# Folding the 64-token turns of a two-layer decoder trunk: Silu, product and split moved to later pieces of weights

## The chip, the cores and the metric

The kernel runs on one core of one Trainium2 chip. The metric is the time of one execution on the device, in microseconds. TensorE (PE in the profile, its weight loads PEld), VectorE (DVE), ScalarE (ACT) and the queue that issues the DMAs (SP) each run their own list of instructions in order and meet through semaphores.

## The reference, cut to what matters

The program computes two decoder layers over 256 tokens of width 1024 in float32. The change touches the last block alone, a top-2-of-8 expert SwiGLU with 3584 hidden units to an expert:

```python
def swiglu(t, w_gate, w_up, w_down):
    return (jax.nn.silu(t @ w_gate) * (t @ w_up)) @ w_down

def moe_swiglu(t, router, w_gate, w_up, w_down):
    ...
    for e in range(N_EXPERTS):
        out = out + combine[:, e:e + 1] * swiglu(t, w_gate[e], w_up[e], w_down[e])
```

All products keep float32 accuracy: every weight and every hidden value is split into a high part (rounded to the float32r format) and a low part (what the rounding left), and the products of the parts are added up.

## The kernel before

**Turns.** The experts are ordered by their token counts and take turns, alternately a large turn (L, up to 128 tokens) and a small one (S, up to 64 tokens): `KIND = "LSLSLSLS"`. Each turn goes through 7 chunks of 512 hidden units. A chunk takes twelve pieces of weights of 128x1024: eight in `gate_up` (four for the gate, then four for the up product, here g0 to g7) and four in `down` (f0 to f3). The order on the engines is software-pipelined: `gate_up` of the next chunk, then `down` of this one, then `gate_up` of the one after.

**A piece.** `split_raw` splits it: ScalarE casts the high part `whi` (L189), VectorE subtracts the low part `wlo` (L190). Both lie in the pool `whl`, with three buffers each. `piece()` splits the piece two ahead before it hands out the next one. So in program order the split of g2 stands ahead of TensorE's products of g0; and as the third buffer is that of the piece just used, this cast waits until TensorE has read the high part of f3, the piece before g0. In an S turn a piece takes four matmuls of 512 columns (`mm2`, L1480 and L1481: the high part, the low part, twice), in an L turn six (`mm3`, L193 to L195).

**The fold of an S turn.** In S turns the left operand holds 64 tokens' high parts in columns 0 to 63 and their low parts in columns 64 to 127, so that two matmuls do what three do in an L turn. The sum of the two halves is then owed. It is done per chunk by `fold`: ScalarE copies the gate and up sums out of PSUM (L1503), TensorE turns and adds the halves with 16 matmuls against the matrix `fold` (`turned`, L1524), ScalarE takes Silu (L1528), VectorE multiplies (the product, L1531), and the result is split into the hidden operand `mhh`: ScalarE's cast (the high part, L189), VectorE's subtraction (the low part, L190). There are 28 folds, seven in each of the four S turns.

**When a step runs.** `after(n, f)` puts a step on a list; `tick()` is called after each piece's products and runs what is due. For a fold made at the end of a `gate_up`, ticks 1 to 4 come after f0 to f3 of the `down` that follows, ticks 5 to 12 after g0 to g7 of the next `gate_up`. The hidden operand of this fold is read in the `down` behind that. The other guest of these ticks is `combine`, which at the start of each turn adds the finished turn's result to `h` (casts `yh`, subtractions `yl`, sums into `h` at L1581), and `dispatch`, which gathers the next turn's tokens during the last `down` but one (`sel`, `xT`, `x`, `sT`). The first fold of an S turn falls into the last `down` of the L turn before it, the last one into the `down` with the dispatch of the L turn behind it.

`in_order` ties the instructions of each of TensorE, ScalarE and VectorE to the order of the program.

Of the kernel before, what the change touches and what calls it, by code (L numbers as in the profile page):

```python
# [10 lines left out]
F32 = mybir.dt.float32  # L11
# [6 lines left out]
OP = mybir.AluOpType  # L18
# [93 lines left out]
def _build(tc, nc, es, I, out, dbg, upto):  # L112
# [28 lines left out]
    def ps(shape, name, tag="ps"):  # L141
        return banks[tag].tile(shape, F32, name=name, tag=tag)
# [45 lines left out]
    def split_to(hi, lo, src):  # L188
        nc.scalar.copy(out=hi, in_=src)  # L189
        nc.vector.tensor_tensor(out=lo, in0=src, in1=hi.bitcast(F32), op=OP.subtract)  # L190
# [25 lines left out]
    def C(k):  # L216
        for offs, t in ((_COFF, cst), (_LOFF, csl), (_KOFF, csk)):
            if k in offs:
                o, n = offs[k]
                return t[:, o:o + n]  # L220
# [9 lines left out]
    def preload(func, after=None):  # L230

        after = eps if after is None else after.bitcast(F32)
        nc.scalar.activation(dummy, after, func, bias=eps, scale=0.0)
# [330 lines left out]
    with ExitStack() as l0:  # L564
# [272 lines left out]
        def finish(p, table=False):  # L837

            if not ya:
                ya.append(Blocks(4, "ya", b4))  # L840
            Yc = c4(Y[p])
            st = rt.tile([128, 3, 4], F32, name="st")
            nc.vector.tensor_scalar(st[:, 0, :], mv[p][:, :, 1], 64e-5, None, op0=OP.add)
            if table:
                nc.scalar.activation(st[:, 2, :], st[:, 0, :], AF.Sqrt)
            nc.vector.tensor_tensor(out=Yc, in0=Yc, in1=mv[p][:, :, 0:1].to_broadcast([128, 4, 64]), op=OP.subtract)
            if table:
                nc.vector.reciprocal(st[:, 2, :], st[:, 2, :])
            else:
                rsqrt(st[:, 2, :], st[:, 0, :], st[:, 1, :])  # L850
            bd = blockdiag("KR")[:, 0]
            for s in halves:
                nc.vector.tensor_tensor(out=bd[s, :, s], in0=Yc[s],
                                        in1=st[s, 2, :, None].to_broadcast([64, 4, 64]), op=OP.mult)
            yield
            g = ps([128, 4, 128], "yT", f"pp{p % 2}" if table else "ps")
            for c in range(4):
                nc.tensor.transpose(g[:, c, :], bd[:, c, :], ident)
            y_ = b1("yl")
            for s in halves:  # L860
                nc.vector.scalar_tensor_tensor(c4(y_[s]), g[s, :, s], V("lg", p)[s], c4(bonus[p][s]),
                                               op0=OP.mult, op1=OP.add)
            yield
            nc.vector.tensor_tensor(out=y_, in0=y_, in1=gg[p], op=OP.mult)
            hi, lo = ya[0](p)
            split_to(hi, lo, y_)
            yield
# [135 lines left out]
        end = [finish(2, True), finish(3, True)]  # L1003
# [21 lines left out]
    with ExitStack() as l0:  # L1025
# [47 lines left out]
        t = unp.tile([128, 2, D], F32, name="un")  # L1073
# [142 lines left out]
    t = unp.tile([128, 2, D], F32, name="un")  # L1216
# [140 lines left out]
    def experts(kinds, late=None, hook=None):  # L1357
# [6 lines left out]
        def after(n, f):  # L1364
            deferred.append([n, f])
# [117 lines left out]
        def gate_up(e, fc):  # L1483
            large = kinds[e] == "L"
            acc = []
            sums = {}
            for w in range(2):
                a = ps([128, 512], "gu", "gu")
                for i in range(4):
                    wh, wl = piece()  # L1490
                    for k in range(2):
                        kb = 2 * i + k
                        c = slice(k * 512, (k + 1) * 512)
                        if large:
                            mm3(a, (X[e][:, 0, kb, :], X[e][:, 1, kb, :]), (wh[:, c], wl[:, c]), kb == 0, kb == 7)
                        else:
                            mm2(a, X[e][:, kb, :], (wh[:, c], wl[:, c]), kb == 0, kb == 7)
                    tick()
                    next(side[0], None)
                acc.append(a)  # L1500
                if not large:
                    t = sums[w] = mt.tile([128, 512], F32, name=("msg", "mhl")[w], **({} if w else {"bufs": 1}))
                    after(1, lambda t=t, a=a: nc.scalar.copy(out=t, in_=a))  # L1503
            end = (e, fc) == (last, NFC - 1)
            if not large:
                return fold(sums, end)
            sgt = mt.tile([128, 512], F32, name="msg", bufs=1)
            nc.scalar.activation(sgt, acc[0], AF.Silu)
            if end:
                preload(AF.Sqrt)  # L1510
            nc.vector.tensor_tensor(out=sgt, in0=sgt, in1=acc[1], op=OP.mult)
            return sgt

        def fold(sums, end):

            H = mt.tile([128, 4, 128], F32R, name="mhh")
            t = mt.tile([128, 512], F32, name="mhl").rearrange("p (w f t) -> p w f t", w=2, f=4)
            pt = []

            def turned():  # L1520
                pt.append(ps([128, 2, 4, 64], "hT", "hT"))
                for w in range(2):
                    for f in range(4):
                        nc.tensor.matmul(pt[0][:, w, f, :], lhsT=sums[w][:, f * 128:(f + 1) * 128], rhs=C("fold"),  # L1524
                                         start=True, stop=True)

            def silu():
                nc.scalar.activation(t[:, 0], pt[0][:, 0], AF.Silu)  # L1528
                if end:
                    preload(AF.Sqrt)  # L1530
                nc.vector.tensor_tensor(out=t[:, 1], in0=t[:, 0], in1=pt[0][:, 1], op=OP.mult)  # L1531
            after(2, turned)
            after(3, silu)
            after(4, lambda: split_to(H[:, :, 0:64], H[:, :, 64:128], t[:, 1]))
            return H

        def hidden_T(sgt):
# [238 lines left out]
```

## Time and profile before

| | us |
|---|---|
| median of 3 runs | 1544.46 (1542.99 to 1547.32) |
| the profiled execution | 1547.44 |
| its span, from the first to the last instruction | 1545.6 |
| VectorE busy | 1251.6 (81%) |
| ScalarE busy | 1055.4 (68%) |
| TensorE busy, matmuls | 1465.9 (95%) |

A row of a timeline gives the start, the time busy, the engine, the line, the operation, what it writes and reads, and how many alike were merged; in brackets stands the idle time before it and what ended that. Neighbouring rows of one engine overlap by about 0.1 us, so the cost of an instruction in a full queue is read from start to start. "mhl" names three tiles in S turns: the copy of the up sums, and the tile with Silu and the product.

### The profile page before, as it was taken

Reading aid. Unit: us, or ns where it says so; the run is one execution under the profiler, and the core shown is the slowest. Engines: PE = TensorE matmul, PEld = TensorE weight load, DVE = VectorE, ACT = ScalarE, POOL = GpSimd, SP = SyncE. Lnnn points to the kernel's source line nnn. Section 1 sums busy time; section 2 is a strip of 40 time slices with the busy share of each in tenths; the row PEclk is TensorE's granted clock in tenths of the full one; section 3 lists DMA queues with packets and bytes.
Section 4 is the critical chain, followed back from the end, with each engine's and each line's share of the span. In section 5 each row is a group of like instructions: output and inputs, shape, how many; then the busy total and the mean of one; then the engine's idle time right before and its main releaser. Section 6 shows DMA issues by size and latency. Waiting matters only on the chain. (4 is left out here: it accounts for less than half of the span.)

```text
span 1545.6 us, 22475 instructions
## 1 busy us (share of the span) xinstructions
PE 1465.9 (95%) x7781; PEld 1190.0 (77%) x7781; DVE 1251.6 (81%) x1634; ACT 1055.4 (68%) x1440; POOL 85.6 (6%) x154
## 2 busy tenths in 40 slices
PE   7889899999999999999999999999999999999995
PEld 6879888998788887776677886677887668887663
DVE  6686865554576568989989989989998999998995
ACT  5644345444455568778887778888777887777884
POOL 4223110001010010000000000000000000000000
PEclk9999999999999999999999999999999999999997
DMA  8230025558553869999999999999998999999941
GB/s 292 76 105 19 1 94 182 186 181 290 161 190 123 312 222 352 340 332 353 409 374 364 381 353 342 391 406 358 354 376 323 384 409 354 363 376 332 369 185 32
DMA packets 78276, 426.86 MB, mean 276 GB/s; under 512 B 9200, under 2 KB 9472, under 8 KB 42560
## 3 DMA queue, kind: packets, MB, share of 16 engines
q1 hardware_dynamic: 77328, 422.38, 73.5%
q0 software_dynamic: 816, 2.87, 0.6%
q8 instruction: 65, 1.06, 0.3%
q14 instruction: 67, 0.55, 0.1%
HBM read 424.15 MB, written 1.05 MB: 275 GB/s over the span
## 5 line engine op out<-in xcount | busy, mean ns | idle before, releaser
L190 DVE TENSOR_TENSOR wlo<-mraw,whi 128x1024 fp32r<-128x1024 f32 x556 | 659.3, 1224 | 61.0 <-ACT whi L189 42.4
L189 ACT CAST whi<-mraw 128x1024 fp32r<-128x1024 f32 x556 | 574.3, 1050 | 123.3 <-PE gu L194 53.8
L190 DVE TENSOR_TENSOR wlo<-raw,whi 128x1024 fp32r<-128x1024 f32 x232 | 280.1, 1223 | 107.1 <-ACT whi L189 102.3
L189 ACT CAST whi<-raw 128x1024 fp32r<-128x1024 f32 x232 | 240.6, 1043 | 124.0 <-PE acc L194 37.9
L1481 PE MATMUL gu<-wlo,x 128*128 128x512 f32 x448 | 194.3, 434 | 21.1 <-DVE wlo L190 19.5
L195 PE MATMUL gu<-wlo,x 128*128 128x512 f32 x448 | 176.6, 394 | 2.1 <-DVE wlo L190 2.0
L1480 PE MATMUL gu<-whi,x 128*128 128x512 f32 x448 | 176.6, 394 | 0.0
L193 PE MATMUL gu<-whi,x 128*128 128x512 f32 x448 | 175.9, 393 | 0.1
L194 PE MATMUL gu<-whi,x 128*128 128x512 f32 x448 | 175.7, 392 | 0.1
L1481 PEld LDWEIGHTS gu<-wlo,x 128*128 128x128 f32 x448 | 83.9, 187 | 99.9 <-DVE wlo L190 86.1
L195 PEld LDWEIGHTS gu<-wlo,x 128*128 128x128 f32 x448 | 84.1, 188 | 25.2 <-DVE wlo L190 7.3
L193 PE MATMUL cp<-u,whi 128*128 128x256 f32 (+1 forms) x360 | 101.9, 283 | 0.0
L194 PE MATMUL cp<-u,wlo 128*128 128x256 f32 (+1 forms) x360 | 101.8, 283 | 0.0
L195 PE MATMUL cp<-u,whi 128*128 128x256 f32 (+1 forms) x360 | 101.8, 283 | 0.0
L193 PEld LDWEIGHTS gu<-whi,x 128*128 128x128 f32 x448 | 84.2, 188 | 18.9 <-ACT whi L189 0.8
L194 PEld LDWEIGHTS gu<-whi,x 128*128 128x128 f32 x448 | 84.2, 188 | 18.6 <-DVE x L190 0.4
L1481 PE MATMUL Y<-wlo,mhh 128*128 128x512 f32 x224 | 94.2, 421 | 3.6 <-DVE wlo L190 3.6
L1480 PE MATMUL Y<-whi,mhh 128*128 128x512 f32 x224 | 92.5, 413 | 2.7 <-DVE mhh L190 2.7
L1480 PEld LDWEIGHTS gu<-whi,x 128*128 128x128 f32 x448 | 84.4, 188 | 11.7
L193 PE MATMUL Y<-whi,mhh 128*128 128x512 f32 x224 | 91.6, 409 | 0.0
L195 PE MATMUL Y<-wlo,mhh 128*128 128x512 f32 x224 | 88.3, 394 | 0.8 <-DVE wlo L190 0.8
L194 PE MATMUL Y<-whi,mhl 128*128 128x512 f32 x224 | 87.7, 392 | 0.0
(435 smaller groups left out, 2461.7 us busy)
## 6 DMA issues: line engine op xcount, KB each, us to landing
mraw<-in_moe SPq DMA_DIRECT2D x277, 1024.0 KB, 6.9
raw<-in_moe SPq DMA_DIRECT2D x116, 512.0 KB, 6.5
raw<-in_ffn_gu SPq DMA_DIRECT2D x44, 512.0 KB, 3.4
raw<-in_w_in SPq DMA_DIRECT2D x38, 512.0 KB, 3.6
raw<-in_ffn_d SPq DMA_DIRECT2D x22, 512.0 KB, 3.5
raw<-in_w_out SPq DMA_DIRECT2D x16, 512.0 KB, 3.7
raw<-in_w_in SPq DMA_DIRECT2D x4, 416.0 KB, 9.3
h<-in_x SPq DMA_DIRECT2D x2, 512.0 KB, 6.7
```

The source lines that it names most:

```text
L189: nc.scalar.copy(out=hi, in_=src)
L190: nc.vector.tensor_tensor(out=lo, in0=src, in1=hi.bitcast(F32), op=OP.subtract)
L193: nc.tensor.matmul(o, lhsT=a[0], rhs=b[0], start=start, stop=False)
L194: nc.tensor.matmul(o, lhsT=a[1], rhs=b[0], start=False, stop=False)
L195: nc.tensor.matmul(o, lhsT=a[0], rhs=b[1], start=False, stop=stop)
L1480: nc.tensor.matmul(o, lhsT=a, rhs=b[0], start=start, stop=False)
L1481: nc.tensor.matmul(o, lhsT=a, rhs=b[1], start=False, stop=stop)
```

## The change

The one closure with Silu and product becomes two (`silu`, `times`), and the split becomes two (`high`, `low`). In every fold but the very last, the fold's matmuls run at tick 3 in place of 2, Silu at 5 in place of 3, the product at 6 in place of 3, the high part at 7 and the low part at 8 in place of 4. In the very last fold (`end`) the ticks stay as they are. No instruction is added, dropped or resized.

```diff
                 nc.scalar.activation(t[:, 0], pt[0][:, 0], AF.Silu)
                 if end:
                     preload(AF.Sqrt)
+
+            def times():
                 nc.vector.tensor_tensor(out=t[:, 1], in0=t[:, 0], in1=pt[0][:, 1], op=OP.mult)
-            after(2, turned)
-            after(3, silu)
-            after(4, lambda: split_to(H[:, :, 0:64], H[:, :, 64:128], t[:, 1]))
+
+            def high():
+                nc.scalar.copy(out=H[:, :, 0:64], in_=t[:, 1])
+
+            def low():
+                nc.vector.tensor_tensor(out=H[:, :, 64:128], in0=t[:, 1], in1=H[:, :, 0:64].bitcast(F32), op=OP.subtract)
+            for n, f in zip((2, 3, 3, 4, 4) if end else (3, 5, 6, 7, 8), (turned, silu, times, high, low)):
+                after(n, f)
             return H
```

## Rows read from the trace of the kernel before

**Rows 1.** The page's list of engines: busy time, share of the span, instructions.
```profile
PE 1465.9 (95%) x7781; PEld 1190.0 (77%) x7781; DVE 1251.6 (81%) x1634; ACT 1055.4 (68%) x1440; POOL 85.6 (6%) x154
```

**Rows 2.** Who waited for whom between 940 and 1045 us, most of the second S turn: us in total, times, the longest.
```profile
PEld gu L1481 <- DVE wlo L190: 18.8, 35, 1.2
DVE wlo L190 <- ACT whi L189: 7.2, 9, 1.4
ACT whi L189 <- PE gu L1480: 5.2, 10, 0.8
ACT mhl L1528 <- PE hT L1524: 5.2, 6, 1.0
PEld Y L1481 <- DVE wlo L190: 4.7, 11, 1.0
```

**Rows 3.** The same between 825 and 925 us, inside the second L turn.
```profile
ACT whi L189 <- PE gu L194: 15.1, 40, 0.8
ACT whi L189 <- PE Y L194: 9.2, 22, 2.1
DVE wlo L190 <- ACT whi L189: 3.6, 8, 1.9
PEld gu L195 <- DVE wlo L190: 0.2, 1, 0.2
```

**Rows 4.** The waits of SP's queue over the whole span, the first row.
```profile
SPq L1188 <- DVE wlo L190: 545.9, 244, 9.5
```

**Rows 5.** Busy time in stretches from one fold's first matmul to the next one's (for the first row, from one transpose to the next in an L turn): the stretch, its length, then PE, PEld, DVE, ACT and POOL with their instructions, granted clock, DMA share, GB/s.
```profile
871.20:888.10 16.90, 16.90 (x77) 13.89 (x76) 15.69 (x15) 13.47 (x15) 0.00 (x0) 1.00 0.98 375
939.60:957.90 18.30, 16.12 (x74) 11.95 (x73) 16.67 (x18) 14.83 (x19) 0.00 (x0) 1.00 0.97 346
957.90:974.40 16.50, 15.18 (x69) 11.02 (x68) 15.62 (x17) 13.41 (x16) 0.00 (x0) 1.00 0.96 354
974.40:989.70 15.30, 14.93 (x65) 10.10 (x64) 14.44 (x15) 13.50 (x17) 0.00 (x0) 1.00 0.97 403
989.70:1005.00 15.30, 14.91 (x65) 10.09 (x64) 14.42 (x15) 13.53 (x17) 0.00 (x0) 1.00 1.02 414
1005.00:1020.70 15.70, 14.93 (x66) 10.10 (x65) 14.84 (x17) 13.56 (x17) 0.00 (x0) 1.00 1.01 409
1039.30:1057.80 18.50, 18.02 (x89) 14.51 (x88) 16.76 (x17) 15.02 (x19) 0.00 (x0) 1.00 0.88 327
```

**Rows 6.** VectorE's timeline around one fold of the last S turn.
```profile
1450.06 5.79 DVE L190 TENSOR_TENSOR wlo<-mraw,whi 128x1024 fp32r<-128x1024 f32 x5
1455.76 0.42 DVE L1531 TENSOR_TENSOR mhl<-mhl,hT 128x256 f32<-128x256 f32 x1
1457.03 1.23 DVE L190 TENSOR_TENSOR wlo<-mraw,whi 128x1024 fp32r<-128x1024 f32 x1 [0.85 <-ACT whi L189]
1458.17 0.42 DVE L190 TENSOR_TENSOR mhh<-mhl,mhh 128x256 fp32r<-128x256 f32 x1
1458.51 10.33 DVE L190 TENSOR_TENSOR wlo<-mraw,whi 128x1024 fp32r<-128x1024 f32 x9
```

**Rows 7.** ScalarE's timeline around the same fold.
```profile
1452.40 1.99 ACT L189 CAST whi<-mraw 128x1024 fp32r<-128x1024 f32 x2
1455.20 0.39 ACT L1528 ACTIVATE mhl<-hT 128x256 f32<-128x256 f32 x1 [0.81 <-PE hT L1524]
1455.95 1.05 ACT L189 CAST whi<-mraw 128x1024 fp32r<-128x1024 f32 x1 [0.36 <-PE Y L1480]
1456.90 0.40 ACT L189 CAST mhh<-mhl 128x256 fp32r<-128x256 f32 x1
1457.21 2.94 ACT L189 CAST whi<-mraw 128x1024 fp32r<-128x1024 f32 x3
1460.56 2.18 ACT L189 CAST whi<-mraw 128x1024 fp32r<-128x1024 f32 x2 [0.41 <-PE gu L1480]
```

**Rows 8.** TensorE's timeline around the same fold: f1 up to 1453.27, the fold's matmuls, f2 from 1454.97; then g1's third and g2's second matmul.
```profile
1453.04 0.39 PE L1481 MATMUL Y<-wlo,mhh 128*128 128x512 f32 x1
1453.27 1.00 PE L1524 MATMUL hT<-csk,msg 128*128 128x64 f32 x8
1454.11 1.06 PE L1524 MATMUL hT<-csk,mhl 128*128 128x64 f32 x8
1454.97 0.48 PE L1480 MATMUL Y<-whi,mhh 128*128 128x512 f32 x1
1455.52 0.40 PE L1480 MATMUL Y<-whi,mhh 128*128 128x512 f32 x1
...
1458.65 0.39 PE L1480 MATMUL gu<-whi,x 128*128 128x512 f32 x1
...
1459.78 0.51 PE L1481 MATMUL gu<-wlo,x 128*128 128x512 f32 x1 [0.28 <-DVE wlo L190]
```

**Rows 9.** ScalarE at the start of a dispatch, and the last matmul of the up sums on TensorE before it.
```profile
1033.48 0.39 PE L1481 MATMUL gu<-wlo,x 128*128 128x512 f32 x1
...
1036.82 0.58 ACT L189 CAST x<-xT 128x512 fp32r<-128x512 f32 x1 [2.09 <-PE xT L1400]
1037.30 0.59 ACT L1503 COPY mhl<-gu 128x512 f32<-128x512 f32 x1
```

**Rows 10.** VectorE and ScalarE around the first fold of the second S turn, with the combine of the L turn before.
```profile
942.02 0.42 DVE L1531 TENSOR_TENSOR mhl<-mhl,hT 128x256 f32<-128x256 f32 x1
943.84 1.23 DVE L190 TENSOR_TENSOR wlo<-mraw,whi 128x1024 fp32r<-128x1024 f32 x1 [1.40 <-ACT whi L189]
945.92 2.35 DVE L190 TENSOR_TENSOR wlo<-raw,whi 128x1024 fp32r<-128x1024 f32 x2
949.92 0.75 DVE L1581 SCALAR_TENSOR_TENSOR h<-cmb,route,h 128x512 f32<-128x512 f32 x1
950.58 3.49 DVE L190 TENSOR_TENSOR wlo<-raw,whi 128x1024 fp32r<-128x1024 f32 x3
...
942.76 1.05 ACT L189 CAST whi<-mraw 128x1024 fp32r<-128x1024 f32 x1 [0.77 <-PE Y L194]
```

**Rows 11.** VectorE at the fifth fold of the second S turn, where the dispatch picks its tokens (`sel`).
```profile
1009.93 0.42 DVE L190 TENSOR_TENSOR mhh<-mhl,mhh 128x256 fp32r<-128x256 f32 x1
1010.27 0.48 DVE L1392 TENSOR_SCALAR sel<-iota,route 128x128 f32<-128x128 int16 x2
1010.66 3.49 DVE L190 TENSOR_TENSOR wlo<-mraw,whi 128x1024 fp32r<-128x1024 f32 x3
```

## The prediction

> **What bounds the kernel now.** The page's list of engines comes first: no engine is the bound by its share alone, TensorE's 95% being of modelled ends [rows 1]. So the waits are read by stage. In an S turn TensorE's loads and matmuls wait for VectorE's low parts (18.8 us and 4.7 us in 105 us), and VectorE waits 7.2 us for casts, nine times, about 0.8 us each [rows 2]. In an L turn it is the other way round: ScalarE waits for TensorE to release a buffer, and TensorE waits 0.2 us in 100 us [rows 3]. The DMAs follow: SP's queue waits for buffers that VectorE frees [rows 4]. So an S turn goes at VectorE's pace, an L turn at TensorE's.
>
> The stretches from fold to fold show it in time: 15.30 us where nothing else runs, 16.50 and 18.30 us with the combine, 15.70 us with the dispatch's picks, 18.50 us in the dispatch, where TensorE is busy for 18.02 us [rows 5].
>
> The timelines of one fold show what the 15.30 us consist of. In a full queue one subtraction follows the other after 1.14 us ((10.33 - 1.22)/8); the cast that follows the high part of the fold, and so the subtraction behind the low part, come 0.34 us later (1458.17 to 1458.51); and between product and next subtraction lie 1.27 us (1455.76 to 1457.03), of which the profile shows 0.85 as idle [rows 6]. 12 x 1.14 + 0.34 + 1.27 = 15.29 us, the stretch. So VectorE's queue is the whole period, and the product lies inside the hole of 1.27 us: it costs nothing.
>
> Where does the hole come from? The fold's 16 matmuls hold TensorE from 1453.27 to 1454.97, 1.70 us [rows 8]. The three buffers are full by then. VectorE works them off (f2, f3, g0, until 1455.76), and the next cast, g1's, waits for f2's buffer: f2's third matmul starts at 1455.52 and takes 0.40, the cast starts at 1455.95, after 0.36 us of idle time ended by that matmul, and VectorE follows 1.08 us later [rows 7, 8]. Silu ran from 1455.20 to 1455.59 and was over before [rows 7]. So the hole belongs to TensorE's block of 1.70 us and to the depth of three, not to Silu.
>
> **The change, part by part.** Nothing is added, so all cost lies in where things stand in the two queues.
>
> *The fold's matmuls, one piece later.* The block of 1.70 us now stands between f2 and f3. The same three full buffers, the same release one piece later: the hole moves from before g1 to before g2 and stays 1.27 us. 0 us.
>
> *The product.* It leaves the hole and stands between the subtractions of g3 and g4, where VectorE is the bound: +0.34 us. That is the start-to-start cost of its twin, the low part, of the same shape and busy 0.42 like it [rows 6]. The low part was paid before and still is: 0.
>
> *Silu.* It now stands behind g2's cast, the first after the hole, ahead of g3's. Small ACT work there takes 0.31 us (1456.90 to 1457.21), a cast 0.945 in a queue, and VectorE starts 1.08 us after a cast's start [rows 7]. Through ScalarE g3's subtraction comes 0.945 + 0.31 + 1.08 = 2.34 us after the start of g2's cast, through VectorE 1.08 + 1.14 = 2.22. The larger holds: +0.12 us. Before, the high part stood in that place, and the low part's 0.34 on VectorE covered it.
>
> *The high part.* ScalarE runs ahead of VectorE. It reaches the high part behind g4's cast, 2 x 0.945 = 1.89 us after the start of g3's cast; the product starts 1.08 + 1.14 = 2.22 us after it and takes 0.42. So ScalarE, in order, stands waiting for about 0.78 us, and behind the high part stands g5's cast, for which VectorE waits next. From the product's start, g5's subtraction comes through ScalarE after 0.42 + 0.03 + 0.31 + 1.08 = 1.84 us, through VectorE's own queue after 0.34 + 1.14 = 1.48: +0.36 us. In the old order the product was over at 1456.18, 0.72 us before ScalarE came to the high part [rows 6, 7], so this wait is new. That a ready instruction does wait behind one that isn't, a dispatch shows: the up sums were done at 1033.87, and their copy ran at 1037.30, right behind the cast of `x` that had idled ScalarE for 2.09 us [rows 9].
>
> The Trainium skill ("Perfetto Trace Analysis", section "Tensor Engine Instruction (MATMUL, LD_WEIGHTS)") states that ACT and DVE work as strict FIFOs; the trace agrees, with those 3.4 us of a ready copy, and by the rule the 0.36 us stand, while with a queue that let g5's cast pass they would be 0.
>
> After the low part VectorE is the bound again, as ScalarE has 0.945 us of work to VectorE's 1.14 a piece, and the two copies of sums fit in as they do now; a slower S turn asks less of the DMAs. Plain period: 15.30 + 0.34 + 0.12 + 0.36 = 16.12 us.
>
> *By fold*, counted first to seventh in each S turn:
> - third, fourth and sixth in four turns, and the fifth in the last turn, which has no picks: 13 x 0.82 = 10.7 us;
> - second: two sums into `h` remain, one between the subtractions of g2 and g3, which covers Silu's 0.12: 4 x 0.70 = 2.8 us;
> - fifth in three turns: the picks (1010.27 to 1010.66, 0.39 us) stand behind f3's ticks [rows 11]; with the hole moved behind g1 they fall into it: 3 x (0.82 - 0.39) = 1.3 us;
> - first: g2's cast waits as before for f3, which starts at the same time (f1, f2 and the block swap only). That is 942.76 + 6 x 0.23 = 944.14, an estimate from the cast of rows 10 and the 0.23 pitch of rows 8; VectorE then has g2 at 945.22 instead of 945.92, a gain of 0.70, and later pays the product 0.34, the low part 0.34 and Silu 0.12. The 0.36 is covered by a sum into `h` (0.66 start to start [rows 10]): 4 x 0.10 = 0.4 us;
> - seventh: it moves into a dispatch and the L chunk behind it, where TensorE is busy 18.02 of 18.50 us and an L piece leaves VectorE 16.90/12 - 1.14 = 0.27 us free [rows 5]: 0. The very last is not changed.
>
> Sum: 10.7 + 2.8 + 1.3 + 0.4 = 15.2 us. On the profiled execution's own time: 1547.4 + 15.2 = 1562.6; that execution lies 3.0 us above the median of the runs, so on the median 1559.7. I say 1560.
>
> **Bounds.** Each wait on ScalarE may be covered by something the rows don't show: without the 0.36 (20 folds) and the 0.12 (16) the product alone is left, 20 x 0.34 minus the picks' 1.2 = 5.6 us, 1550. On the other side the first and the seventh folds may pay the full 0.82 too and the picks cover nothing: 8 x 0.82 - 0.4 + 1.2 = 7.4 us more, 1567.
>
> **The rivals.**
>
> *Silu makes the hole (faster).* The profile books 0.81 us of idle ScalarE before Silu [rows 7] and 5.2 us of such waits in a turn [rows 2]. If g1's cast were late because of it, taking Silu away would close 0.93 us of the hole (1.27 less the product) in 20 folds: -18.6 us, 1526. Against it: ScalarE is idle again for 0.36 us behind Silu, until TensorE's matmul. It decides if Silu ended after 1455.92, when f2's matmul does; it ended 0.33 us before. 0.08.
>
> *No collision of high part and product (product alone).* If ScalarE reached the high part after the product, as it does now, only the product's 0.34 would be left: 5.6 us, about 1550. Against it: the 2.05 us from a subtraction's start to the start of the cast three pieces on (1458.51 to 1460.56 [rows 6, 7]) put ScalarE well ahead of VectorE. 0.13.
>
> *It does nothing.* If the spread work found VectorE idle elsewhere, as it would if S turns went at TensorE's pace: 1544.5. Against it: TensorE waits for VectorE in every piece [rows 2, 8]. 0.06.
>
> *The edges pay too.* 1567; the condition is that the dispatch's casts of `x` come later behind the moved steps. 0.07. My forecast keeps 0.66.
>
> **How the numbers follow.** The likeliest case gives 1560. 1550 to 1567 takes in most of the second rival and of the last, and leaves out the faster one, the one without effect and the tails: about 0.8. A measurement of this kernel tells about 0.3% (4.6 us) from no change. Slower by more than that: 0.66 + 0.07 + 0.11 = 0.84; within it 0.06 + 0.02 = 0.08; faster 0.08.
>
> **What the changed profile would show.** Plain stretches from fold to fold of 16.1 us in place of 15.3; L stretches still 16.9. On VectorE a hole of about 1.2 us ahead of g2's subtraction with no product in it, and a second one of about 0.3 ahead of g5's, ended by a cast. On ScalarE some 0.75 us of idle time before the cast of `mhh`, ended by the product. Wrong would be: stretches of 14.4 us (the hole gone, Silu was the cause), 15.65 (no collision) or 15.3.

## The result and the profile after

The changed kernel takes 1557.65 us (median of 4 runs, 1556.63 to 1558.59) against 1545.62 us for the kernel before beside it (4 runs, 1542.99 to 1547.32): ratio 1.0079, 95% interval 1.0062 to 1.0097, so 9.6 to 15.0 us slower, 12.0 by the medians. The prediction was 1560, slower. Its direction and its mechanism held; the measured amount is a fifth under the forecast one.

The page's list of engines after, to set beside [rows 1]: the same instruction counts, the same busy times within 0.5%.
```profile
PE 1472.5 (95%) x7781; PEld 1191.2 (77%) x7781; DVE 1254.6 (81%) x1634; ACT 1053.2 (68%) x1440; POOL 85.9 (6%) x154
```
No engine has more to do. The time is lost between instructions, and only in S turns. Busy time by stretches after, with the columns of [rows 5]: one of an L turn, then of the second S turn those from the first, second, third and seventh fold.
```profile
874.00:890.90 16.90, 16.90 (x78) 13.88 (x77) 15.69 (x15) 13.48 (x15) 0.00 (x0) 1.00 0.98 380
942.40:960.50 18.10, 16.09 (x72) 11.32 (x71) 16.68 (x18) 14.73 (x19) 0.00 (x0) 1.00 0.92 347
960.50:977.80 17.30, 15.51 (x70) 10.91 (x69) 15.79 (x17) 13.51 (x17) 0.00 (x0) 1.00 0.98 367
977.80:993.80 16.00, 15.06 (x65) 10.08 (x64) 14.51 (x15) 13.36 (x16) 0.00 (x0) 1.00 0.99 385
...
1045.40:1062.60 17.20, 16.74 (x82) 13.67 (x81) 15.58 (x16) 14.14 (x18) 0.00 (x0) 1.00 0.90 343
```
The plain stretch grew from 15.30 to 16.05 us (product to product 16.05 in the timeline below) at nearly the same busy time of VectorE (14.44 and 14.51 us): what was added is idle time. The L stretch is 16.90 as before. From the first fold to the seventh the turn takes 1045.4 - 942.4 = 103.0 us, before 99.7. These stretches begin and end with the fold's own matmuls, which the change moves by one piece, 16.90/12 = 1.4 us in an L chunk. So some 1.4 us move from behind the last fold of a turn to ahead of its first; that is why the last row, up to the next L turn's transpose, is 1.3 us shorter and no gain.

Where the idle time lies shows in VectorE's timeline around one plain fold of the last S turn, after; it answers [rows 6].
```profile
1467.16 2.45 DVE L190 TENSOR_TENSOR wlo<-mraw,whi 128x1024 fp32r<-128x1024 f32 x2 [1.19 <-ACT whi L189]
1469.53 0.41 DVE L1533 TENSOR_TENSOR mhl<-mhl,hT 128x256 f32<-128x256 f32 x1
1469.86 1.22 DVE L190 TENSOR_TENSOR wlo<-mraw,whi 128x1024 fp32r<-128x1024 f32 x1
1471.36 1.22 DVE L190 TENSOR_TENSOR wlo<-mraw,whi 128x1024 fp32r<-128x1024 f32 x1 [0.28 <-ACT whi L189]
1472.50 0.42 DVE L1539 TENSOR_TENSOR mhh<-mhl,mhh 128x256 fp32r<-128x256 f32 x1
1472.84 9.20 DVE L190 TENSOR_TENSOR wlo<-mraw,whi 128x1024 fp32r<-128x1024 f32 x8
...
1485.58 0.41 DVE L1533 TENSOR_TENSOR mhl<-mhl,hT 128x256 f32<-128x256 f32 x1
```
There are two holes where there was one. The first, 1.19 us ahead of g2's subtraction, is the old hole with nothing in it: no product, no Silu. The product now stands between two subtractions that could have followed each other. The second, 0.28 us, is new. ScalarE's timeline of the same fold, after, tells what made it; it answers [rows 7].
```profile
1466.08 1.05 ACT L189 CAST whi<-mraw 128x1024 fp32r<-128x1024 f32 x1 [1.67 <-PE Y L1480]
1467.04 0.38 ACT L1528 ACTIVATE mhl<-hT 128x256 f32<-128x256 f32 x1
1467.31 1.98 ACT L189 CAST whi<-mraw 128x1024 fp32r<-128x1024 f32 x2
1469.97 0.41 ACT L1536 CAST mhh<-mhl 128x256 fp32r<-128x256 f32 x1 [0.68 <-DVE mhl L1533]
1470.29 2.00 ACT L189 CAST whi<-mraw 128x1024 fp32r<-128x1024 f32 x2
```
The idle time before g2's cast is 1.67 us in one piece, ended by TensorE: before, it stood as 0.81 and 0.36 us on either side of Silu. And ScalarE, which had come to the high part at 1469.29 (1467.31 + 1.98), stands 0.68 us until the product is there; g5's cast waits behind it. The waits between 945 and 1050 us, after, beside [rows 2]:
```profile
PEld gu L1481 <- DVE wlo L190: 21.0, 34, 1.4
...
PEld Y L1481 <- DVE wlo L190: 6.6, 16, 1.0
ACT mhh L1536 <- DVE mhl L1533: 4.0, 6, 1.1
```
TensorE waits for VectorE 27.6 us in place of 23.5; the last row, ScalarE for the product, is not among the rows of before.

### The profile page after: what moved, and what is told of

Its sections match the earlier page's. It is cut to its first block, busy times and chain, and to the rows that moved or that the text cites. A ratio compares the mean times of both kernels' runs of the same rounds, so it can differ in the third digit from the quotient of the medians.

```text
span 1555.9 us, 22473 instructions
## 1 busy us (share of the span) xinstructions
PE 1472.5 (95%) x7781; PEld 1191.2 (77%) x7781; DVE 1254.6 (81%) x1634; ACT 1053.2 (68%) x1440; POOL 85.9 (6%) x154
## 5 line engine op out<-in xcount | busy, mean ns | idle before, releaser
L189 ACT CAST whi<-mraw 128x1024 fp32r<-128x1024 f32 x556 | 575.0, 1050 | 135.9 <-PE gu L194 51.5
```

## The experiments

The theory: TensorE's block of 16 matmuls and the depth of three buffers make the hole, wherever the fold stands; the change takes the product out of the hole (price A), puts Silu into a queue without slack (B), and makes ScalarE wait for the product ahead of a cast (C). The chief rival: Silu, or the place of the fold, is behind it. "Stretch" is the time from product to product in the last S turn where nothing else runs, the mean of three in the profiled execution, which agree within 0.03 us: 15.30 us before, 16.05 after. A line of an edit that begins with "..." is cut at its front.

**e1: all of it one piece later, nothing spread (edit against the changed kernel).**
```diff
-... (3, 5, 6, 7, 8), (turned, silu, times, high, low)
+... (3, 4, 4, 5, 5), (turned, silu, times, high, low)
```


> The old arrangement moved one piece later as a whole: ticks 3, 4, 4, 5, 5. Theory (the hole of 1.27 us belongs to TensorE's block and holds the product for free, wherever it stands): the plain stretch from fold to fold is 15.30 us as before the change, the product stands in the hole, and the time is that of the kernel before, or about 1 us less because the picks of three turns fall into the hole. Rival (the loss comes from the fold's matmuls standing one piece later): the plain stretch stays near 16.06 us and the time near +12 us.

Measured 1541.43 us beside 1543.12 for the kernel before, ratio 0.9981 (0.9969 to 0.9993). VectorE around one fold of e1:
```profile
1450.84 0.41 DVE L1533 TENSOR_TENSOR mhl<-mhl,hT 128x256 f32<-128x256 f32 x1
1452.12 1.23 DVE L190 TENSOR_TENSOR wlo<-mraw,whi 128x1024 fp32r<-128x1024 f32 x1 [0.86 <-ACT whi L189]
```
The stretch is 15.29, as before, with the product in the hole and 0.86 us of idle time behind it. So the fold's place costs nothing, and there is even a small gain. The traces put it in two places, counted between VectorE's subtractions of f0, which the edit doesn't move: 0.38 us at each fifth fold with picks, which fall into the hole, as the prediction had it, and 0.33 us at each first fold.

**e2: only Silu at its old distance, the product spread (ticks 2, 3, 5, 7, 8; edit against the changed kernel).**
```diff
-... (3, 5, 6, 7, 8), (turned, silu, times, high, low)
+... (2, 3, 5, 7, 8), (turned, silu, times, high, low)
```


> Ticks 2, 3, 5, 7, 8: matmuls and Silu stay where they were, the product leaves the hole, and the high part comes two ticks behind it, so that it should find the product done. Theory: the plain stretch is 15.30 + 0.34 = 15.64 us, with an empty hole of about 1.2 us and no wait of ScalarE for the product; the time is that of before plus 20 to 24 times 0.34 us, +7 to +8 us. Rival (Silu, not the block, makes the hole, and the product hides anywhere): 15.30 us or less.

Measured 1549.96 us beside 1543.12, ratio 1.0039 (1.0025 to 1.0054), stretch 15.59. VectorE over one period of e2:
```profile
1462.08 2.36 DVE L190 TENSOR_TENSOR wlo<-mraw,whi 128x1024 fp32r<-128x1024 f32 x2 [1.21 <-ACT whi L189]
1464.36 0.41 DVE L1533 TENSOR_TENSOR mhl<-mhl,hT 128x256 f32<-128x256 f32 x1
...
1479.95 0.41 DVE L1533 TENSOR_TENSOR mhl<-mhl,hT 128x256 f32<-128x256 f32 x1
```
The hole is empty (1.21 us of idle time). Price A is 15.59 - 15.30 = 0.29 us, forecast 0.34.

**e3: the changed kernel with two pieces between product and high part (edit against the changed kernel).**
```diff
-... (3, 5, 6, 7, 8), (turned, silu, times, high, low)
+... (3, 5, 6, 8, 9), (turned, silu, times, high, low)
```


> The changed kernel with high and low part one tick later: ticks 3, 5, 6, 8, 9. Theory (in the changed kernel ScalarE waits in order for the product, and g5's cast behind it): that wait and the second hole on VectorE vanish, the plain stretch is 16.06 - 0.36 = 15.70 us, the time 20 x 0.36 = 7 us under the changed kernel, about +5 us on the kernel before. Rival (the loss is the spreading as such): 16.06 us or more.

VectorE and, in the last two rows, ScalarE around one fold of e3:
```profile
1461.17 2.44 DVE L190 TENSOR_TENSOR wlo<-mraw,whi 128x1024 fp32r<-128x1024 f32 x2 [1.19 <-ACT whi L189]
1463.53 0.41 DVE L1533 TENSOR_TENSOR mhl<-mhl,hT 128x256 f32<-128x256 f32 x1
1463.86 3.49 DVE L190 TENSOR_TENSOR wlo<-mraw,whi 128x1024 fp32r<-128x1024 f32 x3
...
1461.32 2.95 ACT L189 CAST whi<-mraw 128x1024 fp32r<-128x1024 f32 x3
1464.17 0.40 ACT L1536 CAST mhh<-mhl 128x256 fp32r<-128x256 f32 x1
```
The high part comes after the product (1463.53 + 0.41 = 1463.94) and waits for nothing; the three subtractions behind the product follow each other. The stretch is 15.67, the time 1549.97 us beside 1543.12 (ratio 1.0041, 1.0025 to 1.0056). So price C is 16.05 - 15.67 = 0.38 us, and price B, Silu, the rest over e2, 15.67 - 15.59 = 0.08 us.

**e4: the fold's eight matmuls of the program spread 2, 1, 1, 2, 1, 1 behind six pieces, Silu and product at 7, high at 9, low at 10 (edit against the changed kernel).**
```diff
+            steps = [(w, f) for w in range(2) for f in range(4)]
+            def turned(n=8):
...
+                for w, f in steps[:n]:
+                    nc.tensor.matmul(pt[0][:, w, f, :], ...)
+                del steps[:n]
...
+                plan = [(1 + i, lambda n=n: turned(n)) for i, n in enumerate((2, 1, 1, 2, 1, 1))]
+                plan += [(7, silu), (7, times), (9, high), (10, low)]
```


> The fold's matmuls themselves are spread: of the eight in the program (16 in the trace) 2, 1, 1, 2, 1, 1 after ticks 1 to 6; Silu and product at 7, high at 9, low at 10; the last fold as before. Theory (the hole is what a block of 1.70 us leaves over VectorE's lead of about 0.43 us): blocks of 0.21 and 0.43 us fit under that lead, the hole goes to nothing, the plain stretch is 12 x 1.14 + 2 x 0.34 = 14.4 us, up to 14.7 if small holes stay, and the time 14 to 22 us under the kernel before. Rival (the hole has another cause, such as Silu or the copies of the sums): a hole of about 1.2 us stays and the plain stretch is 15.6 us, +6 us on the kernel before. Second rival (the DMAs, which had moved 419 GB/s at most, become the bound): ScalarE waits for landings and the stretch stops near 15.0 us.

Measured 1526.99 us beside 1543.12, ratio 0.9896 (0.9876 to 0.9916); stretch 14.73. VectorE's timeline over one period of e4:
```profile
1443.29 0.41 DVE L1536 TENSOR_TENSOR mhl<-mhl,hT 128x256 f32<-128x256 f32 x1
1443.62 3.65 DVE L190 TENSOR_TENSOR wlo<-mraw,whi 128x1024 fp32r<-128x1024 f32 x3
...
1447.52 9.43 DVE L190 TENSOR_TENSOR wlo<-mraw,whi 128x1024 fp32r<-128x1024 f32 x8
...
1458.03 0.41 DVE L1536 TENSOR_TENSOR mhl<-mhl,hT 128x256 f32<-128x256 f32 x1
```
No row has a hole of its own. The same matmuls, Silu and product as in the changed kernel, 1.3 us a fold less: the block makes the hole, not Silu. What is left over a full queue, 0.39 us, is small gaps: 0.16 in the three subtractions behind the product ((3.65 - 1.22)/2 = 1.21 us each in place of 1.14), where ScalarE has the high part and a copy of sums in a row, at 1444.18 and 1444.48, ahead of a cast; and 0.24 in the eight behind ((9.43 - 1.22)/7 = 1.17), at the second tick with two of the program's matmuls.

**e5: the kernel before with the fold's matmuls made twice, the second time to the same place.**
```diff
-                for w in range(2):
-                    for f in range(4):
+                for w, f in [(w, f) for w in range(2) for f in range(4)] * 2:
```


> The kernel before, with every fold's matmuls done twice in a row (the second time over the first result): TensorE's block is 3.40 us in place of 1.70. Theory (the hole is the block less VectorE's lead of 0.43 us): the hole grows by the whole 1.70 us to about 2.97 us with the product still free in it, the plain stretch is 15.30 + 1.70 = 17.0 us, and the time about 28 x 1.7 = 48 us more, as the seventh folds lie in stretches at TensorE's pace. Rival (Silu's or the copies' place on ScalarE sets the hole): the stretch grows by less than 0.5 us, since TensorE has some 2.5 us to spare in 15.3.

One execution: 1595.08 us, beside 1544.76 for the kernel before (median of nine); stretch 17.08. VectorE around one fold:
```profile
1497.55 0.42 DVE L1530 TENSOR_TENSOR mhl<-mhl,hT 128x256 f32<-128x256 f32 x1 [1.56 <-ACT mhl L1527]
1498.97 1.23 DVE L190 TENSOR_TENSOR wlo<-mraw,whi 128x1024 fp32r<-128x1024 f32 x1 [1.00 <-ACT whi L189]
```
The block is 1.70 us longer and the stretch 1.78: once VectorE has no filled buffer left, it stands for what the block grows by. Here VectorE has also to wait for Silu (1.56 us), as the longer block makes Silu late: it is the block that delays Silu and not the reverse.

**e6: one matmul of the program behind each of six pieces, two behind the seventh, Silu and product at 8, high and low at 10 (edit against e4).**
```diff
-... enumerate((2, 1, 1, 2, 1, 1))]
-                plan += [(7, silu), (7, times), (9, high), (10, low)]
+... enumerate((1, 1, 1, 1, 1, 1, 2))]
+                plan += [(8, silu), (8, times), (10, high), (10, low)]
```


> As e4_spread, but the fold's eight matmuls of the program go one each after ticks 1 to 6 and two after tick 7, Silu and product at 8, high and low part at 10. Theory: a step of 0.21 us is what TensorE gains on VectorE in a piece (1.14 less 0.92), so no lag adds up, the 0.35 us of small holes of e4_spread go, and the plain stretch is 14.4 to 14.6 us, the time 3 to 7 us under e4_spread, some 20 us under the kernel before. Rival (the small holes come from the DMAs or from ScalarE's copies): 14.74 us as in e4_spread.

Measured 1519.22 us beside 1544.76, ratio 0.9832 (0.9818 to 0.9845); stretch 14.31. That is VectorE's queue without any gap: twelve subtractions at 1.14 us and two small ones at 0.33 make 14.34.

**e7: the kernel before, with a fourth buffer for the split weights in the expert block and the split run three ahead; the room comes from one of the buffers that the raw weights land in.**
```diff
+        p = whl
+        if deep:
+            p = deep[0] if deep[1] % 4 == 3 else whl
+            deep[1] += 1
...
+            n = n or 1 + AHEAD + bool(deep)
...
-    wraw3 = left(es, "wraw3", NRAW3)
-    ring[:0] = [wraw] * (NWRAW // 2) + [a8p] + [wraw3] * NRAW3
+    deep[:] = [left(es, "whl2", 1), 0]
+    ring[:0] = [wraw] * (NWRAW // 2) + [a8p]
```


> The kernel before with the old ticks, but with a fourth buffer for split pieces in the expert block, split three ahead in place of two; it takes the room of one buffer of the weights' ring. Theory (the hole is the block less the lead that three buffers leave): VectorE has one piece of 1.14 us more to work on, the hole goes from 1.27 to about 0.13 us, the product is paid for, and the plain stretch is 12 x 1.14 + 2 x 0.34 + 0.13 = 14.5 us, the time 14 to 20 us under the kernel before. Rival (the buffers don't set it): 15.3 us.

Measured 1511.80 us beside 1544.76, ratio 0.9789 (0.9774 to 0.9804): the lowest median of all the runs. VectorE over one period of e7 and, in the last row, one cast of ScalarE:
```profile
1441.08 0.41 DVE L1538 TENSOR_TENSOR mhl<-mhl,hT 128x256 f32<-128x256 f32 x1
1441.41 1.21 DVE L196 TENSOR_TENSOR wlo<-raw,whi 128x1024 fp32r<-128x1024 f32 x1
1442.55 0.41 DVE L196 TENSOR_TENSOR mhh<-mhl,mhh 128x256 fp32r<-128x256 f32 x1
1442.91 3.49 DVE L196 TENSOR_TENSOR wlo<-raw,whi 128x1024 fp32r<-128x1024 f32 x3
1446.33 9.16 DVE L196 TENSOR_TENSOR wlo<-mraw,whi 128x1024 fp32r<-128x1024 f32 x8
1455.41 0.41 DVE L1538 TENSOR_TENSOR mhl<-mhl,hT 128x256 f32<-128x256 f32 x1
...
1440.17 1.05 ACT L195 CAST whi<-raw 128x1024 fp32r<-128x1024 f32 x1 [0.37 <-PE Y L1487]
```
The block is whole and the matmuls stand where they stood, and no hole is seen: 14.33 us. What is left of it lies under the product: the cast that starts at 1440.17 lets its subtraction start 1.08 us later, at 1441.25, 0.17 us after the 1441.08 at which VectorE took the product. Block and depth together make it; either remedy is enough. The gain was larger than expected because every fold has it, the first and the seventh too: a turn of S, from the last transpose of the L turn ahead to the first of the one behind, takes 124.1 us in place of 132.0, that is 7 x 0.96 and some 1.2 us in the dispatch. The expected sum had counted the plain folds. Another 2.6 us of the profiled execution's gain lie in the first L turn.

**e8: the change on top of e7.** Against the changed kernel, whose ticks (3, 5, 6, 7, 8) stay, the edit is that of e7:
```diff
+        p = whl
+        if deep:
+            p = deep[0] if deep[1] % 4 == 3 else whl
+            deep[1] += 1
...
+            n = n or 1 + AHEAD + bool(deep)
...
-    wraw3 = left(es, "wraw3", NRAW3)
-    ring[:0] = [wraw] * (NWRAW // 2) + [a8p] + [wraw3] * NRAW3
+    deep[:] = [left(es, "whl2", 1), 0]
+    ring[:0] = [wraw] * (NWRAW // 2) + [a8p]
```


> The change on top of the fourth buffer of e7_deep. Theory (the change loses because the three buffers leave a hole to hide the product in, and 0.3 to 0.4 us of slack on ScalarE; with a fourth buffer the product is paid for in either order and ScalarE's slack is a piece more): the plain stretch is 14.34 us as in e7_deep, and the time that of e7_deep within 2 us. Rival (spreading Silu, product and high part costs 0.8 us a fold in itself): a plain stretch of 15.1 us and 12 to 15 us over e7_deep.

A miss: 1523.09 us beside 1543.23, ratio 0.9864 (0.9846 to 0.9882), some 11 us over e7, stretch 14.93 in place of 14.33. ScalarE and, in the last four rows, VectorE around one fold of e8:
```profile
1434.68 1.05 ACT L195 CAST whi<-mraw 128x1024 fp32r<-128x1024 f32 x1 [1.67 <-PE Y L1487]
1435.64 0.37 ACT L1535 ACTIVATE mhl<-hT 128x256 f32<-128x256 f32 x1
...
1438.57 0.41 ACT L1543 CAST mhh<-mhl 128x256 fp32r<-128x256 f32 x1 [0.68 <-DVE mhl L1540]
...
1434.46 1.22 DVE L196 TENSOR_TENSOR wlo<-mraw,whi 128x1024 fp32r<-128x1024 f32 x1
1435.77 1.23 DVE L196 TENSOR_TENSOR wlo<-mraw,whi 128x1024 fp32r<-128x1024 f32 x1
...
1438.46 1.22 DVE L196 TENSOR_TENSOR wlo<-mraw,whi 128x1024 fp32r<-128x1024 f32 x1
1439.96 1.23 DVE L196 TENSOR_TENSOR wlo<-mraw,whi 128x1024 fp32r<-128x1024 f32 x1 [0.29 <-ACT whi L195]
```
The three prices are all still there, one of them smaller. The fourth buffer gives VectorE work for most of the block, but not for all of it: the first subtraction behind the block starts 1435.77 - 1434.46 = 1.31 us after the one before, 0.17 more than in a full queue. In e7 the product lay over these 0.17 us; spread, it leaves them empty, and so price A is 0.17 in place of 0.29. Silu costs 0.08 as before (the next subtraction comes 1.22 us later, at 1436.98). And ScalarE, late out of the block (1.67 us of idle time in this fold, 1.13 to 1.14 in the three behind it), has no lead over VectorE: the wait for the product costs 1439.96 - 1438.46 - 1.14 = 0.36 us. Together 0.61, and the stretch is 0.60 longer. What had been expected was that a deeper buffer covers both engines.

**e12: e8 with e3's distance, ticks 3, 5, 6, 8, 9 (edit against e8).**
```diff
-... (3, 5, 6, 7, 8), (turned, silu, times, high, low)
+... (3, 5, 6, 8, 9), (turned, silu, times, high, low)
```


> e8_deep_changed with high and low part one tick later (3, 5, 6, 8, 9). Reading of e8 (0.36 of its 0.60 us are the high part's wait for the product, the rest the casts right behind TensorE's block, where Silu stands): the wait goes, the plain stretch falls from 14.94 to 14.58 us, the time 7 us under e8_deep_changed. Rival (the fourth buffer's 0.60 us have one cause, the block's place): 14.9 us stays.

Measured 1514.35 us beside 1544.15, ratio 0.9803 (0.9781 to 0.9825), stretch 14.55: 0.38 us less than e8 and 0.22 more than e7. So the wait for the product was 0.38 us. The rest has no run that splits it; in the trace of e12 it is the same pair as in e8, 0.18 us at the first subtraction behind the block and 0.08 at the next, behind Silu, against some 0.03 of small gaps that e7 has of its own.

**e9: e7 with the low part on GpSimd (but for the very last fold; edit against e7).**
```diff
...
+                nc.gpsimd.tensor_tensor(out=H[:, :, 64:128], in0=t[:, 1], in1=H[:, :, 0:64].bitcast(F32), op=OP.subtract)
...
+                after(4, high)
+                after(4, low)
```


> e7_deep with the fold's low part on GpSimd in place of VectorE (but for the last fold). Theory (with the hole gone VectorE's queue is the whole period, 12 x 1.14 + 2 x 0.34): the plain stretch falls by 0.34 to 14.0 us and the time by 20 to 24 times 0.34, 7 to 8 us, under e7_deep; GpSimd has the time, as its products of this shape took 0.81 to 1.14 us in the kernel before. Rival (GpSimd's accesses slow VectorE's down, or the DMAs bind): 14.3 us or more.

A miss: 1513.83 us beside 1543.23, ratio 0.9804 (0.9786 to 0.9821), stretch 14.50, no better than e7. GpSimd's subtraction takes 1.22 us (1430.25 to 1431.47 in the fold below) and is out of VectorE's queue. But ScalarE waits 0.31 us for the product at the high part, and VectorE then 0.29 us for the cast behind it; the low part on VectorE, 0.33 us, had been lying over just that wait. And the rival has a share: the subtraction that VectorE started while GpSimd's ran took 1.39 us in place of 1.22, which is the 0.17 us that e9 lies over e7.
```profile
1431.16 1.39 DVE L196 TENSOR_TENSOR wlo<-mraw,whi 128x1024 fp32r<-128x1024 f32 x1 [0.29 <-ACT whi L195]
```

**e11: e9 with high and low part one piece later (edit against e9).**
```diff
-                after(4, high)
-                after(4, low)
+                after(5, high)
+                after(5, low)
```


> e9_deep_pool with high and low part at tick 5 in place of 4, two ticks behind the product. Theory (GpSimd's gain of 0.34 us was eaten by ScalarE, which waits for the product at the high part and holds up the next cast by 0.36): that hole on VectorE vanishes, the plain stretch goes from 14.50 to about 14.1 us, the time 7 us under e9_deep_pool. Rival (GpSimd's accesses slow VectorE down): 14.5 us stays.

A miss of another kind: 1567.47 us beside 1544.88, ratio 1.0152 (1.0135 to 1.0169). GpSimd, VectorE and TensorE around one fold of e11, in the profiled execution, which with 1555.87 us is the shortest of the five:
```profile
1460.09 10.88 POOL L1540 TENSOR_TENSOR mhh<-mhl,mhh 128x256 fp32r<-128x256 f32 x1 [13.45 <-ACT mhh L1543]
...
1458.96 11.43 DVE L196 TENSOR_TENSOR wlo<-mraw,whi 128x1024 fp32r<-128x1024 f32 x10
1473.79 1.23 DVE L196 TENSOR_TENSOR wlo<-raw,whi 128x1024 fp32r<-128x1024 f32 x1 [3.40 <-ACT whi L195]
...
1471.03 0.79 PE L1487 MATMUL Y<-whi,mhh 128*128 128x512 f32 x1 [4.15 <-POOL mhh L1540]
```
The gap in VectorE's queue is closed, as wanted: ten subtractions at (11.43 - 1.22)/9 = 1.13 us. But the small one on GpSimd that started among them took 10.88 us and ended at 1470.97, after VectorE had run dry at 1470.39. TensorE waits for it 4.15 us before the `down` pieces, ScalarE for TensorE, VectorE for ScalarE. That happened in eight of the 27 folds on GpSimd, the third and the sixth of each turn; in the other nineteen the subtraction took 0.9 to 1.8 us.

**e10: fourth buffer, spread matmuls (2, 1, 1, 1, 2, 1) and the low part on GpSimd, all together (edit against the changed kernel; the lines of the fourth buffer and of `turned` are those of e7 and e4).**
```diff
...
+                (nc.vector if end else nc.gpsimd).tensor_tensor(out=H[:, :, 64:128], in0=t[:, 1], in1=H[:, :, 0:64].bitcast(F32), op=OP.subtract)
...
+                plan = [(1 + i, lambda n=n: turned(n)) for i, n in enumerate((2, 1, 1, 1, 2, 1))]
+                plan += [(7, silu), (7, times), (9, high), (9, low)]
```


> Fourth buffer, the fold's matmuls spread over ticks 1 to 6, Silu and product at 7, high part two ticks behind at 9, low part on GpSimd at 9. Theory: no hole is left and VectorE's queue is 12 x 1.14 + 0.34 = 14.0 us a plain stretch; the time 5 to 10 us under e7_deep (1511.8). Rival (the DMAs, which would have to move 6.29 MB in 14.0 us, 449 GB/s, over the 419 seen at most, bind): casts wait for landings and the stretch stops at 14.3 us or more.

Measured 1550.27 us beside 1544.88, ratio 1.0030 (1.0016 to 1.0044), where a gain had been expected. The same thing as in e11: GpSimd's subtraction took 6.88 us in eight folds, and TensorE's loads waited for it up to 4.6 us at a time. That neither the transfers nor TensorE was the bound in the forms without GpSimd is shown by e6 and e7, at VectorE's 14.3 us.

## Why the prediction was right

*The hole belongs to the block and the depth.* Right, and shown three ways: it stays at 1.19 to 1.21 us with nothing in it (after, e2, e3), it grows with the block (e5), and it goes with the block spread (e4, e6) or, but for 0.17 us, with a fourth buffer (e7, e8). The rival "Silu makes the hole" would have had 14.4 us after; it was 16.05.

*The fold one piece later costs nothing.* Right: e1.

*The product, +0.34.* 0.29 by e2, nearly its whole 0.33 us from start to start.

*Silu, +0.12.* 0.08, by e3 over e2. The forecast took 0.31 us for a small ScalarE step from start to start [rows 7]; Silu took 0.27 (1467.04 to 1467.31), and 0.12 - 0.04 is 0.08.

*The high part, +0.36.* 0.38 by after over e3. The forecast had 0.78 us of ScalarE's waiting, the trace 0.68; what matters is what comes through ScalarE from the product's start, and there forecast (1.84) and trace (1469.53 to 1471.36, 1.83) agree. The rival of no collision is out: it would be e3's kernel. The strict order in ScalarE's queue on which this step leaned ("Perfetto Trace Analysis" of the Trainium skill, section "Tensor Engine Instruction (MATMUL, LD_WEIGHTS)") is borne out by the pair of after and e3, 0.38 us apart with the high part one place further back in that queue.

*The plain period.* 16.12 forecast, 16.05 measured: 0.75 for 0.82.

*By fold.* The stretches of [rows 5] start at the fold's own matmuls, which the change moves, by a longer piece in an L chunk than in an S one; they make the first fold look 0.2 us shorter. So the folds are counted between places that stay, VectorE's subtractions of f0 in one `down` and the next, in the two profiled executions. The means over the turns are, first to seventh: +0.08 (forecast 0.10), +0.72 (0.70), +0.77 and +0.76 (0.82), +0.37 with picks (0.43: the picks do fall into the hole) and +0.74 without (0.82), +0.77 (0.82), and 0.00 to -0.09 for the seventh (0). So every row of the list held within 0.1 us, the first and the seventh too.

*The sum.* Counted in this way the experts take 14.0 us longer, where 15.2 were forecast. Most of the difference is the price of a plain fold, some 0.76 for 0.82 in 13 folds, and the small gains at the seventh. The medians differ by less, 12.0 us, and why is not shown. Their interval, 9.6 to 15.0, takes in the 14.0; and the five sets of runs of the kernel before that stand beside the experiments have medians of 1543.1 to 1544.9 us, 0.7 to 2.5 under the 1545.62 that the change was measured against. The two profiled executions differ by only 10.3 us, and that lies in stretches that the change doesn't touch: in the one of before, the stages ahead of the experts took 2.0 us more, the very last matmuls ran at half clock (below), 1.16 us, and the stretch behind VectorE's last instruction was 0.54 us longer. How often the half clock falls into the runs that were only timed, no run shows.

## What to carry over

Where one engine lays a solid block in front of a ring of buffers, work out how long the next engine can live on what is filled: here 1.70 us of block left 1.27 us of hole at a depth of three and 0.17 at four, which the product filled, and one buffer gave 33 us. Small steps of the consumer belong into such a hole as long as it is there: spreading them "more evenly" over a full queue left the hole empty and made the product cost 0.29 of its 0.33 us. A step on an in-order engine that needs a result of another must stand far enough behind it: one piece too early cost 0.38 us a time, with ScalarE 32% idle over the span.

## What the runs showed of the hardware

**GpSimd beside a full VectorE.** The same GpSimd subtraction over all of e9 and all of e11, grouped (shortest, median, longest in ns):
```profile
L1540 POOL TENSOR_TENSOR mhh<-mhl,mhh x27: 1208/1217/1481, 701.8 to 1473.8; 128x256 fp32r<-128x256 f32 x27
```
```profile
L1540 POOL TENSOR_TENSOR mhh<-mhl,mhh x27: 872/1721/10894, 701.4 to 1514.0; 128x256 fp32r<-128x256 f32 x27
```
In e9, where VectorE's queue had its gap of 0.29 us at most of these folds, it took 1.2 to 1.5 us each time; in e11, where that gap is closed, up to 10.9 us. In the eight folds of e11 that took so long VectorE's own subtractions followed each other after 1.13 us as ever, and each time GpSimd was done 0.58 to 0.59 us after VectorE's queue had run dry; so it was in the eight folds of e10 with 6.88 us. The wait can fall on VectorE too: in the expert block 20 of its subtractions took 1.38 to 1.66 us in e9 and twelve 1.76 to 1.77 in e11, beside one of 1.8 that these runs share with the kernel before; in e7, without GpSimd, all the others took under 1.3. The Trainium skill ("SBUF — State Buffer", section "Who interferes with whom") states that a VectorE instruction with two inputs in SBUF contends with a GpSimd instruction that reads SBUF. The three runs agree, and e10 and e11 show that GpSimd can be the one that waits, over a whole queue of VectorE's. A closed gap is not enough for that: nineteen of e11's 27 folds took 0.9 to 1.8 us all the same, and what sets the eight apart no run here shows. The five executions of e11 took 1555.9 to 1568.3 us, so it also varies from one to the next.

**TensorE's clock at the end.** Before the last matmuls TensorE waits 2.71 us for the last low part, in both kernels alike. Busy time behind that wait, before, with the columns of [rows 5]:
```profile
1521.90:1525.30 3.40, 3.40 (x10) 2.63 (x9) 1.37 (x2) 1.04 (x1) 0.00 (x0) 0.50 0.00 0
```
And after, in 5.10 us that begin with these matmuls:
```profile
1532.90:1538.00 5.10, 4.64 (x17) 3.04 (x17) 2.84 (x4) 2.11 (x3) 0.00 (x0) 1.00 0.01 2
```
The granted clock is 0.50, 1.2 of 2.4 GHz, for 3.4 us before, and 1.00 after; the last 16 matmuls took 5.14 and 3.98 us, from the first one's start to the last one's. The wait is 2.70 to 2.77 us in all fourteen profiles. Behind it the clock falls in seven of them (before, e5, e7, e8, e10 to e12) and stays in seven (after, e1 to e4, e6, e9). What decides between them no run here shows.
